# Join of a hybrid decoder layer: residual rows turned in pairs of blocks, the last output products and the first MLP products put in one fixed TensorE order

## The chip, the cores and the metric

The kernel runs on one core of one Trainium2 chip. The metric is device time in microseconds (us) from the launch's first to its last work on the core; lower is better. The core has TensorE (PE; its weight loads are shown as PEld), VectorE (DVE), ScalarE (ACT), GpSimd (POOL), and SyncE (SP), which here issues nearly all transfers.

## The reference

One decoder layer on 512 tokens of width 1024, with 16 meta tokens ahead of them. What matters here is the place where the two mixing branches meet:

```python
merged = jax.nn.sigmoid(gate_att) * att + jax.nn.sigmoid(gate_rwkv) * rw
h = layer_norm(ALPHA * h + merged @ w_out[l], ln1_g[l], ln1_b[l])
ff = jnp.square(jax.nn.relu(h @ w_ff1[l])) @ w_ff2[l]
h = layer_norm(ALPHA * h + ff, ln2_g[l], ln2_b[l])
```

`att` is windowed attention, `rw` a recurrent time mix over 16 heads, `w_out` is 1024x1024, `w_ff1` 1024x4096 and `w_ff2` 4096x1024.

## The kernel before, in words

All large products keep f32 accuracy by splitting both operands into a rounded high part and a remainder (`whi`/`wlo`, `hhi`/`hlo`, `h1hi`/`h1lo`) and adding three matmuls, high by high, low by high and high by low. A weight tile (128x1024, 512 KB) is read from memory into one of two `wraw` buffers (line 267), rounded by ACT in two halves (L258) and its remainder taken by DVE in two halves (L261). There are three `whi`/`wlo` pairs and a few `wk` tiles that are kept longer. A tile's buffer comes free when its last reader is done, so a weight load waits for DVE, a rounding for PE.

The layer runs as stages over eight pairs of heads (`s` = -1 to 8). In each stage `weave` lays a list of items, each with a due time in us, between the matmuls of "units" (a projection each). TensorE's order is written out this way (`manual_schedule`); the other engines' orders are made by a scheduler from priorities (`ahead(n)` raises one) and are then fixed lists too. Each engine works its list strictly in order.

The last stage (`s == PAIRS`) holds the last pair's recurrence, the second half of its attention (`attend(s - 1, t1=1.0)[4:]`: two turns of the score rows `pt<-sb`, L1160, and the products `av`, L1180), the residual rows `h` rebuilt and written out (L1247, L1248), and, as units, the output projection: `out_unit` computes `acc[b, n]` (traced as `o`, L1273 to L1275), the rows of block `b` (128 tokens) and half `n` of the columns, over the first six of the eight contraction tiles (`q` = 0 to 2, two tiles each). The last two tiles (`q` = 3) need the last pair's merged heads and come behind the stage.

There the join starts: for each block the four last `project_out` steps (L1273 to L1275), and interleaved with them `first_norm(b)`: add the residual (L1522), statistics (L1503, L1511), 1/deviation (L225, and POOL at L226), normalise (L1527), turn the block's 128x1024 rows into columns by eight transposes in two PSUM banks (L1533), scale and shift on ACT (L1536, eight of 128x128), round on ACT (`h1hi`, L1541, two), remainder on DVE (`h1lo`, L1542, two). The first `NORMED = 2` blocks are normed between the output products. From here to the end TensorE's order is the scheduler's.

Then come the MLP's products `up` (L331 to L333): for `f` = 0 to 2 (`SPLITF = 3`) the first 256 tokens and then the second 256, so that work can start when two blocks are normed; all other `f` take 512 tokens at once. Block 3 is normed behind the first two. ReLU and square are at L1581 to L1584. The tiles `zw`, `za`, `sghi`, `sglo` (pool `lz`, read by the low-rank products and the gate) are given back ahead of the join.

Of the kernel before, what the change touches and what calls it, by code (L numbers as in the profile page):

```python
# [78 lines left out]
NORMED = 2  # L79
# [52 lines left out]
def hybrid_layer_kernel(ctx: ExitStack, tc: tile.TileContext, I: dict, out: bass.AP):  # L132
# [32 lines left out]
    p1 = ctx.enter_context(ExitStack())  # L165
    lz = p1.enter_context(tc.tile_pool(name="lz", bufs=1))
# [84 lines left out]
    def split(raw, hi=None, lo=None, n=P):  # L251
        if hi is None:
            hi = wst.tile([P, D], F32R, name="whi", tag="whi", bufs=WB[0])
            lo = wst.tile([P, D], F32R, name="wlo", tag="wlo", bufs=WB[1])
        w = D // 2
        for q in range(2):
            qs = slice(q * w, (q + 1) * w)
            act.copy(hi[:n, qs], raw[:n, qs])  # L258
        for q in range(2):
            qs = slice(q * w, (q + 1) * w)  # L260
            dve.tensor_tensor(lo[:n, qs], raw[:n, qs], hi[:n, qs].bitcast(F32), op=ALU.subtract)  # L261
        return hi, lo

    def load(tiles, i, keep=None):

# [152 lines left out]

        return dense(col, spans, evict, after=lambda: after(s["z"]))

    zw = lz.tile([P, T], F32R, name="zw")
    za = lz.tile([P, T], F32R, name="za")
    sghi = lz.tile([P, SEQ], F32R, name="sghi")
    sglo = lz.tile([P, SEQ], F32R, name="sglo")

    rest = CONST.shape[1]
    nc.sync.dma_start(con[:, w0:rest], I["consts"][:, w0:rest])
# [836 lines left out]
    def load_out(q, n):  # L1264
        wout[q, n] = load("w_out", 2 * q + n)

    def project_out(q, n, b, d):
# [6 lines left out]
        pe.matmul(acc[b, n], mhi[k][:, bs], lo[:, ws], start=False, stop=False)  # L1274
        pe.matmul(acc[b, n], mlo[k][:, bs], hi[:, ws], start=False, stop=last)  # L1275

    def out_unit(n, blocks, asks):

        if n == 0 and blocks[0] == 0:
# [5 lines left out]
        for q in range(KT // 2 - 1):  # L1285
# [4 lines left out]
            if asks[q]:  # L1290
                load_out(*asks[q])


    SS = [{} for j in range(PAIRS)]
# [161 lines left out]
    p1.close()  # L1456
    prw.close()
    fin = ctx.enter_context(tc.tile_pool(name="fin", bufs=1))

# [55 lines left out]
    h1hi = fin.tile([P, KT, SEQ], F32R, name="h1hi")  # L1515
    h1lo = fin.tile([P, KT, SEQ], F32R, name="h1lo")

    def first_norm(b):
        bs = slice(b * P, (b + 1) * P)
        for n in range(2):  # L1520
            ns = slice(n * 512, (n + 1) * 512)
            dve.scalar_tensor_tensor(  # L1522
                res[b][:, ns], res[b][:, ns], ALPHA, acc[b, n], op0=ALU.mult, op1=ALU.add
            )
            half_stats(st1, b, n)
        mean, r = moments(st1, b)
        dve.tensor_scalar(res[b], res[b], mean, r, op0=ALU.subtract, op1=ALU.mult)  # L1527
        for q in range(2):
            tp = new_bank(b, q, "tp")
            full = fin.tile([P, 4, P], F32, name="h1f", tag="h1f", bufs=2)  # L1530
            for d in range(4):
                k = 4 * q + d
                pe.transpose(tp[:, d * P : (d + 1) * P], res[b][:, k * P : (k + 1) * P], ident)  # L1533
            for d in range(4):
                k = 4 * q + d
                act.activation(  # L1536
                    full[:, d, :], tp[:, d * P : (d + 1) * P], AF.Identity,
                    bias=vcol("ln1_b", k), scale=vcol("ln1_g", k),
                )
            ks = slice(4 * q, 4 * q + 4)  # L1540
            act.copy(h1hi[:, ks, bs], full)  # L1541
            dve.tensor_tensor(  # L1542
                h1lo[:, ks, bs], full, h1hi[:, ks, bs].bitcast(F32), op=ALU.subtract
            )

    for b in range(4):
        for n in range(2):
            for d in range(2):
                project_out(KT // 2 - 1, n, b, d)
        if 0 < b <= NORMED:  # L1550
            with ahead(400):
                first_norm(b - 1)
    pps.close()
    pa = ctx.enter_context(tc.tile_pool(name="pa", bufs=1, space=PSUM))
    ffp = ctx.enter_context(tc.tile_pool(name="ffp", bufs=1))


    def finish(b):
# [6 lines left out]
    NF = DFF // P // 2  # L1565
    for half in range(2):
        fx = [ffp.tile([P, NF - KT, SEQ], F32R, name="f" + x, tag="f" + x) for x in ("hi", "lo")]
        fhi, flo = (m + [f[:, k, :] for k in range(NF - KT)] for m, f in zip((mhi, mlo), fx))

        def up(f, w, t0, n, pool_):  # L1570
            hi, lo = w
            ps = pool_.tile([P, 512], F32, name="dps", tag=f"acc{f % 4}")
            ts_ = slice(t0, t0 + n)
            for k in range(KT):
                ks = slice(k * P, (k + 1) * P)
                three(
                    ps[:, :n], hi[:, ks], lo[:, ks], h1hi[:, k, ts_], h1lo[:, k, ts_],
                    first=(k == 0), last=(k == KT - 1),
                )
            r = fin.tile([P, SEQ], F32, name="rl", tag="rl", bufs=2)[:, :n]  # L1580
            act.activation(r, ps[:, :n], AF.Relu)  # L1581
            act.activation(fhi[f][:, ts_], r, AF.Square)
            dve.tensor_tensor(r, r, r, op=ALU.mult)
            dve.tensor_tensor(flo[f][:, ts_], r, fhi[f][:, ts_].bitcast(F32), op=ALU.subtract)  # L1584

        split_f = SPLITF if half == 0 else 0
        if half == 0:

            for b in range(NORMED, 3):
                first_norm(b)  # L1590
            ws = [load("w_ff1", f, ffp if f > 1 else None) for f in range(split_f)]
            for f in range(2):
                up(f, ws[f], 0, SEQ // 2, pa)
            first_norm(3)
            ppr.close()
            pb = ctx.enter_context(tc.tile_pool(name="pb", bufs=1, space=PSUM, side="right"))
            for f in range(2, split_f):
                up(f, ws[f], 0, SEQ // 2, pa)
            for f in range(split_f):
                up(f, ws[f], SEQ // 2, SEQ // 2, pa)  # L1600
        for f in range(split_f, NF):
            up(f, load("w_ff1", half * NF + f), 0, SEQ, pb)
            if half == 0 and f in (6, 10):

                row = rowvec(("ln1_g", "ln1_b")[f // 10], wst, "wraw")
# [70 lines left out]
```

## Time and profile before

| | us |
|---|---|
| median of 3 runs | 999.57 |
| lowest and highest | 995.95, 1003.83 |
| profiled execution | 997.59 |
| its span, first to last instruction | 995.8 |
| PE busy in it | 946.2 |
| DVE busy | 654.3 |
| ACT busy | 469.6 |
| last stage with the first six tiles of the output products | about 556 to 616 |
| join, to the end of `f` = 3 of the first MLP products | about 616 to 660 |

PE is busy for 95% of the span, so only the places where it waits, or runs at a lower granted clock, can give time. A row of the timeline shows the start, the duration, the engine, the line and operation, and in brackets the engine's idle time just before it with what ended it. Matmuls overlap: rows 0.39 us long that start every 0.23 us are a full PE.

### The profile page before, as it was taken

The page shows a single profiled execution, that of the slowest core. Times are in us where ns is not written, and L with a number is a line of the kernel's source. Part 1 is how long each engine was busy: PE and PEld are TensorE (multiplying, and loading weights), DVE is VectorE, ACT ScalarE, POOL GpSimd, SP SyncE. Part 2 cuts the span into 40 slices and gives each one's busy share as a digit, 9 for nine tenths or more (in the row PEclk, how much of TensorE's full clock was granted, in tenths as well). Part 3 has the DMA queues.
Part 4 walks back from the last instruction along what each step waited for, and adds up shares of the span by engine and source line. Part 5 has one row for each costly group of instructions (what it writes and reads, how often), then busy time and mean ns, then how long its engine had stood idle before and what let it go on. Part 6 is the DMA issues. An engine that isn't in the chain of part 4 may idle for free.

```text
span 995.8 us, 19206 instructions
## 1 busy us (share of the span) xinstructions
PE 946.2 (95%) x7533; PEld 790.8 (79%) x7533; DVE 654.3 (66%) x1503; ACT 469.6 (47%) x1238; POOL 43.4 (4%) x108
## 2 busy tenths in 40 slices
PE   4999899999999999999998999899999999999996
PEld 3988788888888887878886677788888888888885
DVE  8577688787887878778867865766433234543437
ACT  6535448465584575745736822843422124442220
POOL 2000000010010000100001000100000000000001
PEclk9999899999999999999999999899999999999999
DMA  7544332433224432233444535133232323323232
GB/s 269 94 126 125 99 81 67 126 76 104 76 50 124 104 112 68 70 109 88 129 124 104 171 106 212 64 106 127 86 106 74 117 86 104 95 95 100 71 105 84
DMA packets 82674, 105.47 MB, mean 106 GB/s; under 512 B 47766, under 2 KB 54664, under 8 KB 82584
## 3 DMA queue, kind: packets, MB, share of 16 engines
q1 hardware_dynamic: 81088, 102.16, 35.1%
q10 hardware_dynamic: 1496, 2.08, 0.6%
q8 instruction: 59, 0.97, 0.4%
q14 instruction: 31, 0.25, 0.1%
HBM read 86.29 MB, written 13.74 MB: 100 GB/s over the span
## 4 chain that ended last, share of the span: by engine, by line
PE 69%; DVE 17%; ACT 8%; issue 2%; DMA 2%; SPq 0%; POOL 0%; DVEq 0%; ACTq 0%; POOLq 0%
PE dps L331 12%; PE dps L332 11%; PE dps L333 11%; PE acc L1486 6%; PE acc L1488 6%; PE acc L1487 6%; DVE wlo L261 2%; ACT Z L744 2%; PE sc L659 2%; PE o L1273 2%; PE av L1180 2%; DVE AX L884 2%; PE o L1275 1%; PE o L1274 1%; DVE Xf L768 1%
## 5 line engine op out<-in xcount | busy, mean ns | idle before, releaser
L261 DVE TENSOR_TENSOR wlo<-wraw,whi 128x512 fp32r<-128x512 f32 x242 | 159.4, 685 | 175.3 <-ACT whi L258 174.9
L258 ACT CAST whi<-wraw 128x512 fp32r<-128x512 f32 x242 | 141.8, 618 | 274.3 <-PE dps L332 135.2
L331 PE MATMUL dps<-hhi,whi 128*128 128x264 f32 (+1 forms) x640 | 219.1, 342 | 3.4 <-DVE ftmp L764 1.4
L332 PE MATMUL dps<-hlo,whi 128*128 128x264 f32 (+1 forms) x640 | 204.9, 320 | 1.4 <-DVE hlo L312 1.4
L333 PE MATMUL dps<-hhi,wlo 128*128 128x264 f32 (+1 forms) x640 | 204.1, 319 | 0.4 <-DVE wlo L261 0.4
L331 PEld LDWEIGHTS dps<-hhi,whi 128*128 128x128 f32 x640 | 121.8, 190 | 17.1 <-issue 3.0
L333 PEld LDWEIGHTS dps<-hhi,wlo 128*128 128x128 f32 x640 | 121.4, 190 | 9.1 <-DVE wlo L261 0.6
L332 PEld LDWEIGHTS dps<-hlo,whi 128*128 128x128 f32 x640 | 121.8, 190 | 6.9 <-DVE hlo L312 2.5
L331 PE MATMUL dps<-h1hi,whi 128*128 128x512 f32 (+1 forms) x264 | 100.1, 380 | 3.8 <-ACT h1f L1536 3.8
L332 PE MATMUL dps<-h1lo,whi 128*128 128x512 f32 (+1 forms) x264 | 100.3, 380 | 0.0
L333 PE MATMUL dps<-h1hi,wlo 128*128 128x512 f32 (+1 forms) x264 | 99.9, 379 | 0.0
L331 PEld LDWEIGHTS dps<-h1hi,whi 128*128 128x128 f32 x264 | 50.4, 191 | 12.9 <-ACT h1f L1536 4.1
L332 PEld LDWEIGHTS dps<-h1lo,whi 128*128 128x128 f32 x264 | 50.4, 191 | 9.3 <-DVE h1lo L1542 0.2
L333 PEld LDWEIGHTS dps<-h1hi,wlo 128*128 128x128 f32 x264 | 50.4, 191 | 9.1
L1486 PE MATMUL acc<-whi,hhi 128*128 128x512 f32 x128 | 50.7, 396 | 0.0
L1488 PE MATMUL acc<-whi,hlo 128*128 128x512 f32 x128 | 50.4, 394 | 0.0
L1487 PE MATMUL acc<-wlo,hhi 128*128 128x512 f32 x128 | 50.0, 391 | 0.0
L1486 PE MATMUL acc<-whi,fhi 128*128 128x512 f32 x112 | 43.6, 389 | 0.0
L1487 PE MATMUL acc<-wlo,fhi 128*128 128x512 f32 x112 | 43.6, 389 | 0.0
L1488 PE MATMUL acc<-whi,flo 128*128 128x512 f32 x112 | 43.6, 389 | 0.0
L897 ACT ACTIVATE Z<-ch,PC 64x64 f32<-64x64 f32 x56 | 17.3, 308 | 45.6 <-DVE Z L895 44.3
L744 ACT COPY Z<-vt 64x64 f32<-64x64 f32 x128 | 26.4, 206 | 9.0 <-PE vt L737 7.6
(292 smaller groups left out, 1721.9 us busy)
## 6 DMA issues: line engine op xcount, KB each, us to landing
wraw<-in_w_ff_dram SPq DMA_DIRECT2D x64, 512.0 KB, 3.6
wraw<-in_w_in_dram SPq DMA_DIRECT2D x52, 512.0 KB, 4.1
wraw<-in_w_out_dram SPq DMA_DIRECT2D x8, 512.0 KB, 3.8
xt<-in_x_dram SPq DMA_DIRECT2D x4, 512.0 KB
Nd<-NT SPq DMA_DIRECT2D x16, 128.0 KB, 3.0
bv<-bv SPq DMA_DIRECT2D x8, 256.0 KB
bvm<-bv SPq DMA_DIRECT2D x8, 256.0 KB, 3.4
qs<-qhi SPq DMA_DIRECT2D x16, 128.0 KB, 4.0
```

What stands on the lines that cost most here:

```text
L258: act.copy(hi[:n, qs], raw[:n, qs])
L261: dve.tensor_tensor(lo[:n, qs], raw[:n, qs], hi[:n, qs].bitcast(F32), op=ALU.subtract)
L331: pe.matmul(ps, whi, xhi, start=first, stop=False)
L332: pe.matmul(ps, whi, xlo, start=False, stop=False)
L333: pe.matmul(ps, wlo, xhi, start=False, stop=last)
L659: pe.matmul(scs[e][:, c * P : (c + 1) * P], BK[ER[e], 4 * i + c, :], AXg[ER[e], e, 4 * i + c], start=True, stop=True,)
L744: act.copy(Z[2 * i + cc][64 * (1 - e) : 64 * (1 - e) + 64, e, :], vt[64 * cc : 64 * cc + 64, i * P + e * HD : i * P + (e + 1) * HD],)
L884: dve.tensor_tensor(AXg[:, e, cs], AXg[:, e, cs], gqs[e].rearrange("p (c k t) -> p c k t", c=4, k=2), op=ALU.add,)
L1180: pe.matmul(av[64 * e : 64 * e + 64, (2 * i + n) * P : (2 * i + n + 1) * P], vs[:, 2 * i + n], ps[:, 2 * n + e, :], start=(d == 0), stop=( ...
L1486: pe.matmul(acc[b], xhi[k][:, bs], hi[:, ws], start=first, stop=False)
L1487: pe.matmul(acc[b], xhi[k][:, bs], lo[:, ws], start=False, stop=False)
L1488: pe.matmul(acc[b], xlo[k][:, bs], hi[:, ws], start=False, stop=last)
```

## The change

1. In the last stage the second half of attention is due at 3.0 instead of 1.0 (`t1`), so that its first turn stands behind more output products.
2. The unit of blocks 2 and 3, columns 1, takes the blocks as 3, 2 and ends after four contraction tiles instead of six; the other two come in the join.
3. The weights of MLP product `f` = 0 are loaded in the last stage (`first_up`, due at 17.0) into the four tiles of `lz`, whose pool is kept; this load is ahead of the last two loads of `w_out` in SP's queue. `f` = 1 goes to `wk` tiles, 2 and 3 to `whi`/`wlo` (`SPLITF = 4`).
4. The join is one TensorE order: last products of blocks 0 and 1, the four left over of unit 3, last products of 2 and half of 3, the 16 transposes of blocks 0 and 1 (`turn_rows(0)`), the rest of block 3, then for `f` = 0 to 3 the first 256 tokens with the contraction in two halves; the transposes of blocks 2 and 3 stand in the middle of the second halves.
5. Two blocks share a PSUM bank in the turn, so that ACT's scale and shift take 128x256 (32 become 16) and the roundings cover two contraction tiles of 256 tokens. Blocks 0 and 1 are normalised on ACT (`add_norm`, L1546 of the new file) with one added small DVE step, blocks 2 and 3 on DVE as before.

```diff
-SPLITF = 3
+SPLITF = 4
...
+    def load_pieces(tiles, i, pieces):
+
+        raw = wst.tile([P, D], F32, name="wraw", tag="wraw", bufs=WB[2])
+        nc.sync.dma_start(raw, I[tiles][i])
+        for q in range(2):
+            hi, lo = pieces[0][q], pieces[1][q]
+            qs = slice(q * (D // 2), (q + 1) * (D // 2))
+            act.copy(hi, raw[:, qs])
+            dve.tensor_tensor(lo, raw[:, qs], hi.bitcast(F32), op=ALU.subtract)
+        return pieces
...
-        (1, (2, 3), ((3, 0), (3, 1), None)),
+        (1, (3, 2), ((3, 0), (3, 1))),
...
-                items += attend(s - 1, t1=1.0)[4:] + join(s - 1, 25.5)
+                items += attend(s - 1, t1=3.0)[4:] + join(s - 1, 25.5)
                 items += [(2.0, (), F(merged, s - 2)), (25.6, (), F(merged, s - 1))]
-                items += [(3.0, (), residual_gain)]
+                items += [(3.0, (), residual_gain), (17.0, (), first_up)]
...
+            if b < 2:
+                nm = fin.tile([P, 1], F32, name="fnm", tag=f"fnm{b}")
+                dve.tensor_scalar(nm, mean, r, -1.0, op0=ALU.mult, op1=ALU.mult)
+                act.activation(res[b], res[b], AF.Identity, bias=nm, scale=r)
+            else:
+                dve.tensor_scalar(res[b], res[b], mean, r, op0=ALU.subtract, op1=ALU.mult)
...
+                for d in range(2):
+                    for b in range(2):
+                        pe.transpose(
+                            t4[:, d, b * P : (b + 1) * P],
+                            res[2 * u + b][:, (k + d) * P : (k + d + 1) * P], ident,
+                        )
+                for d in range(2):
+                    act.activation(
+                        full[:, d], t4[:, d], AF.Identity,
+                        bias=vcol("ln1_b", k + d), scale=vcol("ln1_g", k + d),
+                    )
+                act.copy(h1hi[:, k : k + 2, us], full)
...
+        for b in range(2):
+            last_rows(b, 0)
+            last_rows(b, 1)
+        for d in range(2):
+            for b in (3, 2):
+                project_out(KT // 2 - 2, 1, b, d)
+        last_rows(2, 0)
+        last_rows(2, 1)
+        last_rows(3, 0)
+        turn_rows(0)
+        last_rows(3, 1)
...
+        for f in range(SPLITF):
+            up(ps[f], ws[f], first, range(KT // 2))
+        for f in range(SPLITF):
+            if f == 1:
+                turn_rows(1)
...
+            up(ps[f], ws[f], first, range(KT // 2, KT))
+            squared(f, ps[f], first, n)
...
+        for f in range(SPLITF):
+            ps = pb.tile([P, 512], F32, name="dps", tag=f"acc{f}")[:, :n]
+            up(ps, ws[f], second, range(KT))
+            squared(f, ps, second, n)
```

On TensorE, at the start of the last stage, before (`o` with a number is one block's bank, `pt<-con,sb` the turn of the score rows, `up` and `meta` the recurrence):

```order
L1160 MATMUL pt<-con,sb 128x128 x4
L1273 MATMUL o_7692<-whi,hhi 128x512
L1274 MATMUL o_7692<-wlo,hhi 128x512
L1275 MATMUL o_7692<-whi,hlo 128x512
L820 MATMUL up<-XB,U 16x16 x32
L917 MATMUL meta<-RHm,XTm 16x64 x2
L1273 MATMUL o_7693<-whi,hhi 128x512
L1274 MATMUL o_7693<-wlo,hhi 128x512
L1275 MATMUL o_7693<-whi,hlo 128x512
```

On TensorE at the same place, now, from the same `up` on:

```order
L829 MATMUL up<-XB,U 16x16 x32
L926 MATMUL meta<-RHm,XTm 16x64 x2
L1282 MATMUL o_7693<-whi,hhi 128x512
L1283 MATMUL o_7693<-wlo,hhi 128x512
L1284 MATMUL o_7693<-whi,hlo 128x512
L1282 MATMUL o_7692<-whi,hhi 128x512
L1283 MATMUL o_7692<-wlo,hhi 128x512
L1284 MATMUL o_7692<-whi,hlo 128x512
L1169 MATMUL pt<-con,sb 128x128 x4
L844 MATMUL up<-X_7739,NT 32x32 x16
L931 MATMUL meta<-SVm,BTm 64x64 x2
```

The turn moved from ahead of `up<-XB` to behind two steps of output products that follow it, and one step of output products more now stands ahead of `up<-XB`; the recurrence's next step, `up<-X`, follows the turn at once.

On ScalarE at the join, before (`wk` and `whi` are weight roundings, `h1f` the scale and shift, `h1hi` its rounding):

```order
L258 CAST wk<-wraw 128x512 x2
L1536 ACTIVATE h1f<-tp,vc 128x128 x5
L1541 CAST h1hi<-h1f 128x4x128
L1536 ACTIVATE h1f<-tp,vc 128x128 x4
L1541 CAST h1hi<-h1f 128x4x128
```

On ScalarE at the join, now:

```order
L256 CAST wk<-wraw 128x512 x2
L1546 ACTIVATE res_8163<-res_8163,fnm,rsf_8226 128x1024
L256 CAST whi<-wraw 128x512 x2
L1546 ACTIVATE res_8164<-res_8164,fnm,rsf_8250 128x1024
L256 CAST whi<-wraw 128x512
L1565 ACTIVATE h1f<-tp,vc 128x256 x3
L1569 CAST h1hi<-h1f 128x2x256
L1565 ACTIVATE h1f<-tp,vc 128x256
L256 CAST whi<-wraw 128x512
L1569 CAST h1hi<-h1f 128x2x256
```

The two normalisations came to ScalarE, and the roundings of `f` = 2 and 3 now stand between them and the first columns.

On VectorE in the join, now (`res` with a number is a block's residual rows, 8165 block 2 and 8166 block 3):

```order
L1538 SCALAR_TENSOR_TENSOR res_8166<-res_8166,o_7890 128x512
L1526 BN_AGGR fmv<-fst_8173 128x2
L259 TENSOR_TENSOR wlo<-wraw,whi 128x512
L223 TENSOR_SCALAR rsf_8286<-fmv 128x1
L1518 BN_STATS fst_8174<-res_8166 128x6
L1548 TENSOR_SCALAR res_8165<-res_8165,fmv,rsf_8286 128x1024
L1570 TENSOR_TENSOR h1lo<-h1f,h1hi 128x2x256
L1538 SCALAR_TENSOR_TENSOR res_8166<-res_8166,o_8104 128x512
L1570 TENSOR_TENSOR h1lo<-h1f,h1hi 128x2x256
```

The first remainder of the turned rows, `h1lo`, stands behind block 2's normalisation.

More of the change, by code (lines that the diff above doesn't have):

```diff
@@ L78 @@
 HOLD = 4
-NORMED = 2
 SBB = 2
 WB = (3, 3, 2)
-SPLITF = 3
+SPLITF = 4
 PS = (2, 2, 1, 1, 2)
@@ L164, in hybrid_layer_kernel @@
     hpool = ctx.enter_context(tc.tile_pool(name="hpool", bufs=1))
-    p1 = ctx.enter_context(ExitStack())
-    lz = p1.enter_context(tc.tile_pool(name="lz", bufs=1))
+    lz = ctx.enter_context(tc.tile_pool(name="lz", bufs=1))
     prw = ctx.enter_context(ExitStack())
@@ L419, in shifted @@
         return dense(col, spans, evict, after=lambda: after(s["z"]))
[L421 to L424, printed above, removed]
+    zw = lz.tile([P, T], F32R, name="zw", tag="zw")
+    za = lz.tile([P, T], F32R, name="za", tag="za")
+    sghi = lz.tile([P, SEQ], F32R, name="sghi", tag="sghi")
+    sglo = lz.tile([P, SEQ], F32R, name="sglo", tag="sglo")
     rest = CONST.shape[1]
@@ L1275, in project_out, with first_up @@
         pe.matmul(acc[b, n], mlo[k][:, bs], hi[:, ws], start=False, stop=last)
+    def first_up():
+        A["w1"] = load_pieces("w_ff1", 0, [
+            [lz.tile([P, SEQ], F32R, name="w1", tag=t) for t in tags]
+            for tags in (("zw", "za"), ("sghi", "sglo"))
+        ])
     def out_unit(n, blocks, asks):
-        if n == 0 and blocks[0] == 0:
+        if n == 0 and 0 in blocks:
             with ahead(PRI["dense"]):
@@ L1284, in out_unit @@
             acc[b, n] = new_bank(b, n, f"o{b}{n}")
-        for q in range(KT // 2 - 1):
+        for q, ask in enumerate(asks):
             for d in range(2):
@@ L1289, in out_unit @@
                     yield 3 * 0.227
-            if asks[q]:
-                load_out(*asks[q])
+            if ask:
+                load_out(*ask)
     SS = [{} for j in range(PAIRS)]
@@ L1455, in hybrid_layer_kernel @@
     p2.close()
-    p1.close()
     prw.close()
@@ L1516, in hybrid_layer_kernel @@
     h1lo = fin.tile([P, KT, SEQ], F32R, name="h1lo")
[L1518 to L1523, printed above, removed]
-            )
[L1525 to L1555, printed above, removed]
+    def add_norm(b):
+        with ahead(400):
+            for n in range(2):
+                ns = slice(n * 512, (n + 1) * 512)
+                dve.scalar_tensor_tensor(
+                    res[b][:, ns], res[b][:, ns], ALPHA, acc[b, n], op0=ALU.mult, op1=ALU.add
+                )
+                half_stats(st1, b, n)
+            mean, r = moments(st1, b)
+            if b < 2:
[4 more added lines that the diff above has]
+                dve.tensor_scalar(res[b], res[b], mean, r, op0=ALU.subtract, op1=ALU.mult)
@@ new lines, in turn_rows @@
+    def turn_rows(u):
+        us = slice(u * 2 * P, (u + 1) * 2 * P)
+        with ahead(400):
+            for k in range(0, KT, 2):
+                tp = new_bank(2 * u + k // 2 % 2, k // 4, "tp")
+                t4 = tp.rearrange("p (d t) -> p d t", d=2)
+                full = fin.tile([P, 2, 2 * P], F32, name="h1f", tag="h1f", bufs=2)
+                for d in range(2):
[8 more added lines that the diff above has]
+                        bias=vcol("ln1_b", k + d), scale=vcol("ln1_g", k + d),
+                    )
+                act.copy(h1hi[:, k : k + 2, us], full)
+                dve.tensor_tensor(
+                    h1lo[:, k : k + 2, us], full, h1hi[:, k : k + 2, us].bitcast(F32),
+                    op=ALU.subtract,
+                )
@@ new lines, in hybrid_layer_kernel, with activations, up @@
+    NF = DFF // P // 2
+    ffp = ctx.enter_context(tc.tile_pool(name="ffp", bufs=1))
+    def activations():
+        fx = [ffp.tile([P, NF - KT, SEQ], F32R, name="f" + x, tag="f" + x) for x in ("hi", "lo")]
+        return (m + [f[:, k, :] for k in range(NF - KT)] for m, f in zip((mhi, mlo), fx))
+    fhi, flo = activations()
+    def up(ps, w, ts_, ks):
+        for k in ks:
+            if isinstance(w, list):
+                c = slice(k % 4 * P, (k % 4 + 1) * P)
+                hi, lo = (x[k // 4][:, c] for x in w)
+            else:
+                hi, lo = (x[:, k * P : (k + 1) * P] for x in w)
+            three(
+                ps, hi, lo, h1hi[:, k, ts_], h1lo[:, k, ts_],
+                first=(k == 0), last=(k == KT - 1),
+            )
@@ L1563, in finish @@
             (nc.sync, nc.scalar)[q].dma_start(out[0, b * P : (b + 1) * P, qs], res[b][:, qs])
-    NF = DFF // P // 2
     for half in range(2):
[L1567 to L1602, printed above, removed]
+        if half:
+            fhi, flo = activations()
+        for f in range(0 if half else SPLITF, NF):
+            ps = pb.tile([P, 512], F32, name="dps", tag=f"acc{f % 4}")
+            up(ps, load("w_ff1", half * NF + f), slice(0, SEQ), range(KT))
+            squared(f, ps, slice(0, SEQ), SEQ)
             if half == 0 and f in (6, 10):
```

20 lines of the change are left out of this document (added).

## Prediction

> **What bounds the kernel now.** First the page, for the share of each engine:
>
> ```profile
> PE 946.2 (95%) x7533; PEld 790.8 (79%) x7533; DVE 654.3 (66%) x1503; ACT 469.6 (47%) x1238; POOL 43.4 (4%) x108
> ```
>
> TensorE sets the end, and the change leaves nearly all of its work as it is. So it can save only what TensorE loses between 560 and 660 us, the stretch that it reorders. The waits of TensorE there, all of them (total, times, longest):
>
> ```profile
> PE dps L331 <- ACT h1f L1536: 3.8, 1, 3.8
> PE pt L1160 <- ACT sb L1150: 2.0, 1, 2.0
> PE o L1273 <- ACT z L975: 0.9, 1, 0.9
> ```
>
> That is 6.7 us. Behind a wait the granted clock can fall. The busy times by window (the column behind POOL is the granted clock) and one shorter wait from an earlier stage:
>
> ```profile
> 486.80:490.20 3.40, 1.85 (x9) 1.19 (x9) 3.31 (x9) 3.37 (x10) 0.00 (x0) 1.00 0.27 88
> 562.70:566.50 3.80, 1.80 (x8) 1.07 (x7) 3.80 (x9) 3.80 (x11) 0.00 (x0) 0.94 0.60 180
> 566.50:569.80 3.30, 3.30 (x75) 2.32 (x74) 3.24 (x7) 2.65 (x10) 0.00 (x0) 0.55 0.88 254
> 628.50:632.30 3.80, 0.02 (x1) 0.03 (x1) 3.78 (x8) 3.80 (x11) 0.00 (x0) 0.82 0.02 10
> 632.30:637.70 5.40, 5.40 (x25) 5.40 (x26) 4.96 (x12) 3.25 (x8) 1.48 (x2) 0.50 0.31 95
> ...
> 488.41 0.91 PE L1160 MATMUL pt<-con,sb 128*128 128x128 f32 x3 [1.55 <-ACT sb L1150]
> ```
>
> The wait of 3.8 us was followed by 5.4 us at half clock, that of 2.0 us by 3.3 us at about half (0.55); the wait of 1.55 us at 488 left the clock at 1.00. So two of the three waits cost about double.
>
> **The change part by part.**
>
> *The start of the last stage (`t1` 1.0 to 3.0).* TensorE's rows:
>
> ```profile
> 562.34 0.39 PE L1275 MATMUL o<-whi,hlo 128*128 128x512 f32 x1
> 564.73 1.21 PE L1160 MATMUL pt<-con,sb 128*128 128x128 f32 x4 [2.00 <-ACT sb L1150]
> 570.24 0.69 PE L835 MATMUL up<-X,NT 32*32 32x32 f32 x32
> 571.13 0.44 PE L1180 MATMUL av<-pall,vtok 128*64 128x128 f32 x4
> 572.15 0.66 PE L1160 MATMUL pt<-con,sb 128*128 128x128 f32 x4
> 572.57 0.48 PE L1273 MATMUL o<-whi,hhi 128*128 128x512 f32 x1
> ```
>
> Matmuls of 512 columns start every 0.23 us, so a step of output products (three) is 0.69. A turn of four is 0.42 (572.15 to 572.57), an `up` with its `meta` 0.89 (570.24 to 571.13). From 562.57, when the next instruction could start, to 570.24 the kernel before does one turn, three steps and one `up` with `meta`: 0.42 + 2.07 + 0.89 = 3.4 us of work in 7.7, so 4.3 lost. Now the same pieces stand in the order step, `up`, step, step, turn, and then `up<-X` follows. What they wait for, on ACT and DVE:
>
> ```profile
> 562.72 1.65 ACT L258 CAST whi<-wraw 128x512 fp32r<-128x512 f32 x3
> 564.28 1.87 ACT L1150 ACTIVATE sb<-sb,sm 128x128 f32<-128x128 f32 x6
> 567.74 1.10 ACT L826 COPY XB<-up 16x128 f32<-16x128 f32 x4
> 568.86 0.41 ACT L919 COPY SVm<-meta 16x64 f32<-16x64 f32 x2
> ...
> 568.23 0.89 DVE L830 STREAM_TRANSPOSE X<-XB 32x256 f32<-32x256 f32 x2
> ```
>
> TensorE reaches the turn at 562.57 + 3 x 0.69 + 0.89 = 565.5. ACT is free of roundings at 564.3 and has four `sb` done (0.30 each) at 565.5: the wait of 2.0 goes. But ACT now does `XB` next (1.1, to 566.6), DVE turns it 0.3 later (566.9; before, 568.84 to 569.12), and TensorE is through its turn at 566.0: a new wait of 0.9 at `up<-X`. ACT then has four more `sb` (567.8) and `SVm` (568.0) ahead of the second `meta`, for which TensorE is ready at 567.5: 0.4 to 0.5. Together 1.35 are left of 4.3; both are shorter than the 1.55 that left the clock alone. Gain **2.9**; at the bounds 4.3 (neither wait) and 1.0 (both waits, and a fall of the clock: 3.3 us at half speed lose 1.65, plus 0.3).
>
> *The bank behind `z`.* The next fence holds the rest of TensorE's rows that I use. At 606.86 an `o` waits for ACT to read its bank. Now block 3's step, whose bank is free, stands ahead and covers 0.69 of the 0.93: gain **0.7**.
>
> ```profile
> 606.86 0.50 PE L1273 MATMUL o<-whi,hhi 128*128 128x512 f32 x1 [0.93 <-ACT z L975]
> 627.37 1.09 PE L1533 MATMUL tp<-con,res 128*128 128x128 f32 x8
> 632.28 0.58 PE L331 MATMUL dps<-h1hi,whi 128*128 128x256 f32 x1 [3.81 <-ACT h1f L1536]
> 637.76 0.28 PE L333 MATMUL dps<-h1hi,wlo 128*128 128x256 f32 x1
> 641.35 0.28 PE L333 MATMUL dps<-h1hi,wlo 128*128 128x256 f32 x1
> 641.48 1.03 PE L1533 MATMUL tp<-con,res 128*128 128x128 f32 x8
> 642.27 0.37 PE L331 MATMUL dps<-h1hi,wk 128*128 128x256 f32 x1
> 654.18 0.40 PE L331 MATMUL dps<-h1hi,whi 128*128 128x512 f32 x1
> 659.65 0.39 PE L331 MATMUL dps<-h1hi,whi 128*128 128x512 f32 x1
> ```
>
> *The wait at the join.* Before, TensorE is out of work after the turn at 627.37, and ACT has 16 `h1f` to do. Now I count from T, the start of block 0's last products, with these durations:
>
> ```profile
> 622.12 1.14 ACT L258 CAST wk<-wraw 128x512 fp32r<-128x512 f32 x2 [5.43 <-DMA wraw<-in_w_ff_dram]
> 624.98 1.85 ACT L1536 ACTIVATE h1f<-tp,vc 128x128 f32<-128x128 f32 x5 [1.72 <-PE tp L1533]
> 627.99 1.28 DVE L1522 SCALAR_TENSOR_TENSOR res<-res,o 128x512 f32<-128x512 f32 x2
> ...
> L1527 DVE TENSOR_SCALAR res<-res,fmv,rsf 128x1024 f32<-128x1024 f32 x4 | 3.2, 811 | 0.5 <-POOL rsf L226 0.4
> L241 ACT ACTIVATE xt<-xt,nm,rs 128x1024 f32<-128x1024 f32 x2 | 2.4, 1227 | 0.0
> L1581 ACT ACTIVATE rl<-dps 128x256 f32<-128x256 f32 x6 | 2.4, 393 | 1.3 <-PE dps L333 1.3
> L226 POOL TENSOR_TENSOR rsf<-rsf,mhalf 128x1 f32<-128x1 f32 x4 | 2.6, 648 | 31.7 <-PE o L1275 19.4 <-DVE rsf L225 12.3
> ```
>
> TensorE: 18 steps end at T + 12.5, 16 transposes (eight are 0.79, 641.48 to 642.27) at 14.1, two steps at 15.5. The normalised block 1 is there in time: its second sum can start at 5.7, its statistics end at 8.5; DVE then waits for `f` = 2's rounding, whose buffer is read until 8.4, and ACT (1.23 for a normalisation) has block 1 done at 11.9. The columns: ACT rounds half of `f` = 3 when the 18th step has freed its buffer (12.7 to 13.3), then three `h1f` at 0.4 and `h1hi` at 0.5: 15.1, ahead of 15.5. DVE is later. At 10.7 it turns to block 2, and with 0.6 for each 128x512 (two in 1.28) it does: two sums, the second when its products end at 11.4 (12.1), two statistics (13.3), a sum (13.9), aggregate and `wlo` (14.6), 1/deviation and a statistic (15.3, POOL's 0.65 beside it), the normalisation (0.81; 16.2), and only then `h1lo`: 16.8. `up`'s second matmul waits for it, 1.3 us; the third contraction tile waits 0.5 more for the next `h1lo`, which stands behind one more sum. From there nothing is late by this count (the second turn is reached at 24.4, block 3 is normalised at 22.7). So 1.8 of 3.8 stay: gain **2.0**, bounds 3.8 and, with DVE a whole wait of 3.8 late, 0.
>
> *The clock behind it.* 632.28 to 637.76 are 5.5 us for 16 matmuls of 256 columns (0.12 each) and eight transposes (0.79): 2.7 us of work. Without the long wait the **2.8** are back; bounds 2.8 and 0.
>
> *Two MLP halves more.* `f` = 3 now takes 48 matmuls at 0.12 for 24 in 5.47 us (654.18 to 659.65): −0.3. Four interruptions by transposes become two, about 0.2 each by the rows around them: +0.4. Net **0.1**. The Trainium skill (TensorE: Matmul & The Clock Gate, Back-to-back issue gap) gives sustained 81 ns at 128 columns and 131 ns at 512; a straight line puts 256 near 98, an estimate from that page, and the split at 24 x (196 − 131) = 1.6 us against the change. By that the sum would be 7.2; the rows above decide for 0.3.
>
> *The early load.* `f` = 0 is issued ahead of two loads that have over 8 us to spare; its two roundings (1.14) now stand in ACT's list ahead of the chain's last step:
>
> ```profile
> 597.50 0.31 ACT L897 ACTIVATE Z<-ch,PC 64x64 f32<-64x64 f32 x1 [0.82 <-DVE Z L895]
> ...
> 598.59 0.63 PE L951 MATMUL Y<-Z,AX 128*64 128x64 f32 x14
> wraw<-in_w_ff_dram SPq DMA_DIRECT2D x7, 512.0 KB, 4.2
> ```
>
> They take up the 0.82 us of idle time and 0.3 more; the reader comes 0.8 after `Z` ends. Cost nothing; if the load came a microsecond late, half of that would show.
>
> Sum: 2.9 + 0.7 + 2.0 + 2.8 + 0.1 = 8.5 us. The profiled execution (997.59) would become 989.1. It lies 2.0 below the median of 999.57, inside the spread of the runs, so the forecast for the median is **991.1**.
>
> **The rivals.**
>
> *The clock falls again at the join.* The two new waits, 1.3 and 0.5, lie within 2.6 us of each other, and 1.8 in one stretch is between the 1.55 that was harmless and the 2.0 that was not. Then 3.3 to 5.4 us run at half speed and 1.65 to 2.7 are lost: 992.8 to 993.8. For it: how close 1.8 is to 2.0. Against it: the clock fell only behind waits in one piece. The Trainium skill (same page, Why this matters for your kernels) says that gaps up to about 3 us leave the clock alone. By that this rival could not be. The trace differs: 2.0 us were enough at 564.7.
>
> *The start does not do what it says*: the wait for `sb` only moves to `XB` and `SVm`, and the clock falls there too: the gain is 1.0 for 2.9, so 993.0.
>
> *The count is too careful*: DVE gets to `h1lo` in time and both waits of the stage's start vanish: 991.1 − 1.8 − 1.4 = 987.9.
>
> *Slower than before: ACT's list blocks.* The half rounding of `f` = 3 stands ahead of the first `h1f`. Its load is issued only when DVE has finished `f` = 1 (T + 7.9), and must land by T + 12.7, 4.8 later, where such loads took 4.2. Each microsecond beyond holds up `h1f`, `h1hi`, `h1lo` and TensorE by one, and from about one on the clock falls as well (2.8). It decides from a landing 5.7 us too late, when 5.7 + 2.8 use up the 8.5; at 17 us too late the kernel would stand at 1011. Against it: the transfers have room there, since DMA moved 10 GB/s from 628.5 to 632.3 (the last column of its row).
>
> **How the numbers follow.** As worked out 0.50 (988 to 994, with the spread of runs); clock at the join 0.20; the start gains little 0.13; too careful 0.12; ACT blocked 0.05. The likeliest is 991.1. A median of a few runs moves by some 3 us (the runs lie 3.6 below to 4.3 above theirs), so the range goes from the too careful case less 3, 985, to the two clock cases together (995.7) and a little more, 997. One per cent, about what a measurement here can tell from no change, is 10 us: faster by more needs under 989.6, which the too careful case gives nearly always (0.11), the likeliest in four of ten (0.20), the others sometimes (0.06). Slower by over 1% is the far end of the last case, 0.04. Rounded: 0.37, 0.59, 0.04.
>
> **What would show it.** Right: no wait over 1.5 us on TensorE from 560 to 660, and the clock at 1.00 there; `up<-X` waits for DVE's `X` about 0.9; the first `up` of the MLP waits for `h1lo`, 1 to 1.5; `f` = 4 starts some 8.5 us earlier than 659.65. Wrong: a wait of TensorE on a rounding or a load in the join, a clock of 0.5 behind it, or time lost elsewhere, where the order is unchanged.

## The result

| | median of 20 runs | lowest to highest | profiled execution | its span |
|---|---|---|---|---|
| before | 996.99 us | 994.04 to 1003.83 | 997.59 us | 995.8 us |
| after | 995.92 us | 992.13 to 999.29 | 996.54 us | 994.7 us |

The ratio is 0.9988, with a 95% interval of 0.9977 to 0.9999: about 1 us less, where 991.1 and a gain of 8.5 us in the profiled execution were forecast. The 991.1 set out from 999.57, the median of the three runs that were known of the kernel before; its median over 20 runs is 2.6 lower.

### The profile page after: what moved, and what is told of

It is laid out like the page before. It is cut to its first block, busy times and chain, and to the rows that moved or that the text cites. A ratio compares the mean times of both kernels' runs of the same rounds, so it can differ in the third digit from the quotient of the medians.

```text
span 994.7 us, 19253 instructions
## 1 busy us (share of the span) xinstructions
PE 949.3 (95%) x7557; PEld 790.0 (79%) x7557; DVE 653.1 (66%) x1505; ACT 468.8 (47%) x1226; POOL 44.2 (4%) x108
## 4 chain that ended last, share of the span: by engine, by line
PE 67%; DVE 17%; ACT 9%; DMA 3%; issue 2%; POOL 0%; SPq 0%; DVEq 0%; ACTq 0%; POOLq 0%
PE dps L340 12%; PE dps L341 11%; PE dps L342 11%; PE acc L1501 6%; PE acc L1503 6%; PE acc L1502 6%; DVE wlo L259 2%; ACT Z L753 2%; PE sc L668 2%; PE av L1189 2%; DVE AX L893 2%; PE o L1282 1%; DVE ftmp L773 1%; DVE Xf L777 1%; PE o L1284 1%
## 5 line engine op out<-in xcount | busy, mean ns | idle before, releaser
L341 PE MATMUL dps<-h1lo,whi 128*128 128x512 f32 (+1 forms) x256 | 97.5, 381 | 0.0
L340 PE MATMUL dps<-h1hi,whi 128*128 128x512 f32 (+1 forms) x256 | 97.4, 381 | 0.0
L342 PE MATMUL dps<-h1hi,wlo 128*128 128x512 f32 (+1 forms) x256 | 97.4, 381 | 0.0
L342 PEld LDWEIGHTS dps<-h1hi,wlo 128*128 128x128 f32 x256 | 48.1, 188 | 10.1
L340 PEld LDWEIGHTS dps<-h1hi,whi 128*128 128x128 f32 x256 | 48.1, 188 | 10.0
L341 PEld LDWEIGHTS dps<-h1lo,whi 128*128 128x128 f32 x256 | 48.1, 188 | 10.0
L1601 DVE TENSOR_TENSOR rl<-rl 128x512 f32<-128x512 f32 (+1 forms) x36 | 22.8, 632 | 15.4 <-ACT hhi L1600 9.2
```

Of the source, the lines that this page charges most:

```text
L340: pe.matmul(ps, whi, xhi, start=first, stop=False)
L341: pe.matmul(ps, whi, xlo, start=False, stop=False)
L342: pe.matmul(ps, wlo, xhi, start=False, stop=last)
```

## The profile after

First TensorE's waits from 560 to 660 us in the changed kernel, all of them (total, times, longest). They answer to the three of before:

```profile
PE dps L341 <- DVE h1lo L1570: 1.4, 2, 1.1
PE up L844 <- DVE X L839: 0.7, 2, 0.5
PE meta L931 <- ACT SVm L928: 0.4, 1, 0.4
PE dps L340 <- ACT h1f L1565: 0.3, 1, 0.3
PE o L1282 <- ACT z L984: 0.2, 1, 0.2
```

3.0 us in place of 6.7, and with the same partners as forecast: `up<-X` behind DVE's `X`, `meta` behind `SVm`, the first `up` of the MLP behind `h1lo`. TensorE's own rows (start, duration, the wait in brackets) at the stage's start, at the join, and at the first matmul of `f` = 4:

```profile
565.47 0.60 PE L1169 MATMUL pt<-con,sb 128*128 128x128 f32 x4
566.61 0.22 PE L844 MATMUL up<-X,NT 32*32 32x32 f32 x2 [0.55 <-DVE X L839]
566.99 0.69 PE L844 MATMUL up<-X,NT 32*32 32x32 f32 x30 [0.16 <-DVE X L839]
568.06 0.33 PE L931 MATMUL meta<-SVm,BTm 48*64 48x64 f32 x4 [0.39 <-ACT SVm L928]
...
627.86 0.38 PE L341 MATMUL dps<-h1lo,w 128*128 128x256 f32 x1 [1.13 <-DVE h1lo L1570]
...
653.33 0.40 PE L340 MATMUL dps<-h1hi,whi 128*128 128x512 f32 x1
```

`f` = 4 starts 6.3 us earlier than the 659.65 of before; 8.5 was forecast. The windows (the granted clock is the column behind POOL's busy time) show one half of what is missing there:

```profile
565.44:568.85 3.41, 2.32 (x43) 1.75 (x42) 3.07 (x7) 3.24 (x11) 0.00 (x0) 1.00 0.97 279
568.85:572.26 3.41, 3.41 (x38) 2.42 (x37) 2.87 (x6) 1.83 (x6) 0.00 (x0) 0.50 0.27 104
631.00:638.00 7.00, 7.00 (x63) 7.00 (x63) 3.32 (x7) 2.94 (x8) 0.93 (x1) 1.00 0.50 153
```

At the join the clock stays at 1.00, as forecast (by the clock records from 572.26 to 992.10 us). At the stage's start it falls, though no wait there is longer than 0.55 us. By the starts of four matmuls in the two timelines, the time between them, stage by stage:

```
                                                      before    after    gained   forecast
up to the first output product (561.09, 560.82)                           0.3       -
first product to the 37th (581.34, 580.10)             20.25    19.28     1.0      2.9
37th to block 0's last products (615.28, 610.66),
  less the 12 products (2.8 us) that now stand later   33.94    33.33     0.6      0.7
from there to f = 4, less the same 12                  44.36    39.89     4.5      4.9
f = 4 to the last matmul (987.77, 986.66)             328.12   333.33    -5.2       -
```

So 6.3 us are gained, and 5.2 of them are given back behind 653 us, where the order of work is the old one, TensorE is busy without a gap and the clock is at 1.00 in both. TensorE in the second half of the MLP, before and then after, 50 us by windows (busy time and number of matmuls):

```profile
830.00:880.00 50.00, 50.00 (x222) 41.42 (x221) 25.16 (x38) 21.45 (x39) 0.00 (x0) 1.00 0.30 95
```

```profile
830.00:880.00 50.00, 50.00 (x216) 40.24 (x215) 24.08 (x36) 20.48 (x36) 0.00 (x0) 1.00 0.28 92
```

Six matmuls fewer in the same time. And four in a row, before and then after:

```profile
839.91 0.39 PE L333 MATMUL dps<-h1hi,wlo 128*128 128x512 f32 x1
840.14 0.39 PE L331 MATMUL dps<-h1hi,whi 128*128 128x512 f32 x1
840.37 0.39 PE L332 MATMUL dps<-h1lo,whi 128*128 128x512 f32 x1
840.60 0.39 PE L333 MATMUL dps<-h1hi,wlo 128*128 128x512 f32 x1
```

```profile
839.76 0.39 PE L341 MATMUL dps<-h1lo,whi 128*128 128x512 f32 x1
839.99 0.40 PE L342 MATMUL dps<-h1hi,wlo 128*128 128x512 f32 x1
840.23 0.39 PE L340 MATMUL dps<-h1hi,whi 128*128 128x512 f32 x1
840.46 0.40 PE L341 MATMUL dps<-h1lo,whi 128*128 128x512 f32 x1
```

They start 0.227 us apart before, and 0.23 to 0.24 after. There is no wait in it: a row shows it only in the distance to the next.

What differs is where the tiles lie. `lz` is now never closed, so everything that is allocated behind it lies 8320 bytes higher (two tiles of 528 elements and two of 512, of 4 bytes each; 128 modulo 256), and some small tiles add to that. The place of the tiles in the built programs, modulo 256 bytes (the theory that the experiments test; the traces hold no addresses), with the mean distance of the 512-column matmuls from `f` = 4 on:

```
         weights   h1   f, wk   `up` on h1   last products on f   on merged heads
before     224     224   224     0.2267           0.2267              0.2317
after      224      96   160     0.2329           0.2294              0.2317
```

672 matmuls x 0.0062 + 383 x 0.0027 = 5.2 us: all that was given back.

## The experiments: where the tiles lie

The numbers say in which order they ran.

**1. The pool alone.** The kernel before, with `lz` left open and nothing else:

```diff
-    p1 = ctx.enter_context(ExitStack())
-    lz = p1.enter_context(tc.tile_pool(name="lz", bufs=1))
+    lz = ctx.enter_context(tc.tile_pool(name="lz", bufs=1))
...
-    p1.close()
```

> The kernel before, with one thing of the change: the pool `lz` stays open, so that `h1hi`, `h1lo`, `fhi`, `flo` and `wk` lie 8320 bytes higher; the order of work is the old one. Theory (place): the MLP's matmuls of 512 columns go slower because of where their tiles lie, whatever ran ahead of them: those that read `h1` start 0.232 to 0.233 us apart, not 0.2267, and the kernel takes 4.3 to 6.7 us more than before (4.3 from `h1` alone, 2.4 more if `f` and `wk`, which are now 128 bytes off the weights modulo 256 as `h1` is, do the same). Rival (order): the spacing comes from what the new order of work sets going, its halves and buffers: 0.2267 and no change here. Rival (chance): it differs from one execution to the next: no change on the median.

Measured: 1005.16 us, ratio to before 1.0083 (1.006 to 1.0107), some 7.7 us slower between the medians. The same 50 us:

```profile
830.00:880.00 50.00, 50.00 (x215) 40.20 (x215) 23.70 (x37) 20.06 (x37) 0.00 (x0) 1.00 0.30 95
```

`up` on `h1` is at 0.2329, the last products on `f` (now 128 bytes off the weights, too) at 0.2324; together 6.5 us over 0.2267, inside the interval of 6.0 to 10.7. With the old order, and so without a gain to set against it, the pool costs what the MLP loses. The order of work has no part in it.

**2. The changed kernel, with the tiles put back.**

```diff
+    fin.tile([P, 32], F32, name="gap0")
     h1hi = fin.tile([P, KT, SEQ], F32R, name="h1hi")
...
+    ffp.tile([P, 48], F32, name="gap1")
     fhi, flo = activations()
```

> The changed kernel with two unused tiles of 128 and 192 bytes, ahead of `h1hi` and of `fhi`, which put `h1`, `f` and `wk` on the same place modulo 256 as the weights, as they lay before. Place: spacing of the MLP's matmuls on `h1` and `f` back at 0.2267 us, 5.2 us less than the changed kernel, about 6.3 under the one before: 990.7. Order or chance: spacing 0.232 as in the changed kernel, 996.

Measured: 990.73 us, ratio 0.9941 (0.9923 to 0.996); both distances are 0.2267, and the 50 us hold as many matmuls as before the change:

```profile
830.00:880.00 50.00, 50.00 (x222) 41.40 (x221) 24.84 (x38) 20.68 (x37) 0.00 (x0) 1.00 0.32 96
```

320 bytes that nobody uses bring the change's own gain out.

**3. Everything moved together.** The kernel before:

```diff
+    cst.tile([P, 16], F32, name="gap0")
     wst = ctx.enter_context(tc.tile_pool(name="wst", bufs=2))
```

> The kernel before with an unused tile of 64 bytes ahead of the weights' pool: weights, `hhi`, `hlo`, `h1`, `f` and `wk` all move up by 64 bytes together. Place, in the form that the distance between the two operands of a matmul modulo 256 decides: spacing as before (0.2267 on `h1` and `f`, 0.231 on `hhi`), no change. Place, in the form that each tile's own address decides: slower spacing on `h1` and `f`, 3 to 6 us more.

Measured: 997.91 us, ratio 1.0005 (0.9987 to 1.0023); distances 0.2267, 0.2267 and 0.2317 as before. A shift of 64 bytes that both operands share changes nothing, so it is the place of one against the other that counts, and neither's own.

**5. The merged heads**, on top of the kernel of experiment 2. They lay in rows of 528 elements (2112 bytes), so that the blocks' places modulo 256 go round by 64:

```diff
-    mhi = [hhi[:, k, NMETA:] for k in range(KT)]
-    mlo = [hlo[:, k, NMETA:] for k in range(KT)]
+    mhi, mlo = (
+        [x.rearrange("p k t -> p (k t)")[:, k * SEQ : (k + 1) * SEQ] for k in range(KT)]
+        for x in (hhi, hlo)
+    )
```

> The kernel of the second experiment (changed, `h1` and `f` on the weights' place modulo 256), and the merged heads, too, which are kept in the tiles of `hhi` and `hlo`, now in rows of 512 elements from the tile's start (2048 bytes apart) in place of rows of 528 (2112 apart): every block of them lies on the weights' place modulo 256. Place: the matmuls on them go from 0.2317 to 0.2267 us, 1.9 us less over the MLP's 384, and some 0.8 less over the 192 output products ahead of it: 988.0. Rival: only the tiles' starts matter, not each row's, or what holds up these products is the change of operand tiles from one to the next: 990.7 as in the second experiment.

Measured: 988.62 us, ratio 0.9907 (0.9884 to 0.9929). The last products on the heads are at 0.2267, too (0.2317): the whole MLP now runs at one distance. Twelve us of it, here and in the kernel with the tiles put back:

```profile
730.00:742.00 12.00, 12.00 (x55) 9.94 (x54) 2.59 (x4) 2.28 (x4) 0.00 (x0) 1.00 0.34 113
```

```profile
730.00:742.00 12.00, 12.00 (x53) 9.77 (x52) 3.28 (x6) 2.95 (x6) 0.00 (x0) 1.00 0.30 87
```

The output products ahead of the join gained only 0.2 of the 0.8 expected (from 572 us on, 0.2300 for 0.2317 between products that follow each other), though their rows were moved as well: what holds them up besides is open.

**7. Another distance**, on top of the kernel of experiment 2, one run: the unused tiles at 192 and 320 bytes.

> The kernel of the second experiment with the unused tiles at 192 and 320 bytes, so that `h1` lies 64 bytes behind the weights modulo 256 and `f` and `wk` 192. One look for the spacing by distance, of which 0 and 128 for `h1`, 0, 64 and 128 for `f` are known. Place modulo 256 in any distance: 0.229 to 0.233 on both, 2.5 to 7 us over the second experiment in all. If only 128 bytes apart collide: 0.2267 on both; if places modulo 128 collide, which 64 and 192 share: the same spacing on both.

Measured: 993.27 us. `up` on `h1`, 64 bytes off, is at 0.2289. `f`, 192 bytes behind the weights and so 64 ahead modulo 256, lies where it lies in the changed kernel (160) and showed the same 0.2294, so it says nothing new. In the three distances seen the cost grows: 0.2267 at 0, 0.229 at 64 to either side, 0.233 at 128. It does not give every size: the merged heads of 2112 bytes a row go round by 64, and the mean of the four distances would be 0.2295, where 0.2317 was measured.

## The experiments: the join, the start and the clock

**4. The start alone.** The kernel before with `t1=3.0` in place of 1.0.

> The kernel before with `t1=3.0` for 1.0 alone. By the prediction's count the last stage gains 2.9 us. By its rival 1.0. A third view, from the changed kernel's trace, where the waits went as counted and the clock fell all the same: 2.9 where the clock's window (3.4 us, running on its own) happens not to fall on the stage's sparse stretch, 1.2 where it does, so 1.2 to 2.9 on the median. The MLP's spacing is as before.

Measured: 995.34 us, ratio 0.9981 (0.9963 to 0.9999), about 2 us less. Its waits in the stretch, of which the last two replace the 2.0 for `sb`:

```profile
PE dps L331 <- ACT h1f L1536: 3.8, 1, 3.8
PE o L1273 <- ACT z L975: 0.9, 1, 0.9
PE up L835 <- DVE X L830: 0.7, 2, 0.5
PE meta L922 <- ACT SVm L919: 0.4, 1, 0.4
```

**6. The join without the start.** The kernel of experiment 2 with `t1=1.0`.

> The kernel of the second experiment with `t1` back at 1.0, so the join and the early load without the new start. By the prediction's sum the start is worth 2.9: 993.6. By the fourth experiment's median it is worth 2.1: 992.8. If the two gains share the same clock window or the join gives its part only with the new start: 995 or more.

Measured: 992.86 us, ratio 0.9962 (0.9947 to 0.9976): by the ratio the join is worth 3.8 us (2.4 to 5.3; the medians lie 4.7 apart), where 0.7 + 2.0 + 2.8 + 0.1 = 5.6 were forecast, and the start 992.86 − 990.73 = 2.1 on top, between medians of different rounds.

**What makes the clock fall.** The same wait of 1.55 us for `sb` in the stage before, on which the forecast rested since it left the clock at 1.00, ends in half clock in the kernel of experiment 2:

```profile
487.43 1.21 PE L1169 MATMUL pt<-con,sb 128*128 128x128 f32 x4 [1.55 <-ACT sb L1159]
```

```profile
485.62:489.04 3.42, 1.86 (x9) 1.05 (x8) 3.24 (x11) 3.39 (x11) 0.00 (x0) 1.00 0.27 79
489.04:492.45 3.41, 3.41 (x10) 2.66 (x9) 3.14 (x5) 1.39 (x4) 0.00 (x0) 0.50 0.80 276
```

In the clock records of every trace all changes lie on a grid of 3.413 us that runs through the execution, and begins at another phase in each: in the profile of before they are at 112.08, 566.05, 630.90 and 637.73, and 637.73 − 112.08 is 154.0 x 3.413. So I counted, in each stretch of the grid at full clock, the columns of the matmuls that start in it, as a share of 8192 (a yardstick: products of 512 columns 0.2267 us apart make 0.94 on the mean). In the first nine profiles, from 45 to 980 us:

```
share of 8192 columns   stretches   followed by half clock
under 0.36                  27              27
0.36 to 0.43                19               2
over 0.43                 2379               0
```

The bounds 0.36 and 0.43 were read off these same nine profiles; the three of experiments 8 to 10 are the test, and are told there and at the end. The wait of 1.55 us shows the phase at work: in the profile of before an edge of the grid at 487.54 cuts through it, and the two stretches have 0.63 and 0.50; in the kernel of experiment 2 it lies inside one, which has 0.25.

The stretch 565.44 to 568.85 above has 0.34: a turn, 32 products of 32 columns, and the waits. Busy time doesn't tell it: TensorE is busy for 2.3 of its 3.4 us. The old join leaves under 0.2 in one stretch of all four profiles that have it, and the clock fell in all four; the new one leaves at least 0.38, and it fell in none of the five that have it.

**8. Filling the idle time.** On top of the kernel of experiment 5, products that nothing reads, in three places where TensorE waits:

```diff
+    def fill(ps, n, cols):
+        for i in range(n):
+            pe.matmul(ps[:, :cols], hhi[:, 0, :P], hhi[:, 1, :cols], start=True, stop=True)
...
+                if j == 0:
+                    fill(up, 14, 512)
...
+                if j == PAIRS - 1:
+                    fill(up[:, 256:512], 4, 256)
...
+        if j == PAIRS - 2 and i == 0:
+            fill(pt, 6, 512)
```

> The kernel of the fifth experiment with idle time of TensorE filled at three places by products that nothing reads, written to the bank of the instruction that waits: 14 of 512 columns (3.2 us) ahead of the first `up<-X`, which waits 3.8 us at 110.9 for a transfer; 6 of 512 (1.4 us) ahead of the turn at 489 that waits 1.6 for `sb`; 4 of 256 (0.5 us) ahead of the `up<-X` of the last stage that waits 0.55. Theory (columns): the clock is set on a grid of 3.413 us by the columns that TensorE streamed in the stretch before; in the nine profiles so far all 27 stretches below 0.36 of what a stretch can hold were followed by half clock, 2 of 19 between 0.36 and 0.43, and none of 2379 above. The fills lift these places over 0.43, so that no half clock follows at 107 to 118, 489 to 493 and 566 to 573; what is left is one early fall at 60 to 75 in some executions, and the end. A stretch at half clock costs 1.4 us by the spread of the runs, and about 2.5 of them go: 985, 3 to 4 us under the fifth experiment. Rival (waits): only the length of a wait in one piece counts; then 566 still falls in some executions, and the gain is the same or less. Rival (work): more products are more work, and no faster: 988.6 or more.

Measured: 986.13 us, ratio 0.9877 (0.9855 to 0.9898). The clock is at 1.00 from 31 to 979 us, where the work ends (the column behind POOL's busy time):

```profile
31.00:979.00 948.00, 925.91 (x7499) 777.01 (x7497) 628.67 (x1447) 452.11 (x1194) 37.88 (x79) 1.00 0.36 103
```

The four runs lie within 1.0 us of each other, the six of experiment 5 within 5.3. Against experiment 5 the time is 2.5 us less between the medians, but the two intervals overlap. One stretch at 71.6 went on at full clock with 0.30, the only one under 0.36 that did. The second place is no test here: its products ran elsewhere (see 10), and the stretch of that wait, unfilled, happened to have 0.44.

**9. Busy, but with few columns.** The same three places with 56, 24 and 8 products of 16 columns.

> The same three fills with products of 16 columns, 56, 24 and 8 of them, which keep TensorE as busy for about as long (some 0.055 us each, as the products of 128 columns in the trace), and stream an eighth of the columns or less. Columns: the clock falls as without the fill, at 107 to 118 always and at 489 and 566 to 573 in some executions, 988.6 as in the fifth experiment. Waits or busy time: no fall there, and the time of the filled kernel.

Measured: 993.78 us, ratio 0.9951 (0.9935 to 0.9966). In the first place, TensorE without a gap and at half clock for three stretches:

```profile
108.21:111.62 3.41, 3.41 (x33) 3.41 (x32) 1.82 (x4) 1.08 (x3) 0.00 (x0) 1.00 0.78 145
111.62:121.86 10.24, 10.24 (x112) 9.28 (x112) 2.26 (x5) 0.52 (x2) 0.00 (x0) 0.50 0.23 89
```

So a TensorE that the profile calls busy doesn't hold the clock (the first stretch has 0.06); the 14 products of 512 columns in the same place did. That the time is worse than experiment 5's and not the same is, as far as the rows show, the fill's own doing: I took 0.055 us for a product of 16 columns, and the 56 took 8.3 us, where the wait was 3.8; the 24 ran at 550 and took 2.4, where nothing waits:

```profile
L804 PE MATMUL up<-hhi 128*128 128x16 f32 x56 | 8.3, 292 | 0.0
```

**10. The second fill in its right place.** In the eighth kernel those six products ran at 543, ahead of a turn that waits for nothing, and the turn at 485.60 waited its 1.55 us as ever. With `j == PAIRS - 3`:

> The kernel with the three fills, the second of which stood ahead of a turn at 543 that waits for nothing, and so was 1.4 us of added work; now it stands ahead of the turn that waits 1.55 us for `sb` in the stage before. Columns: the clock stays at 1.00 as with the first filled kernel, that turn waits 0.2 instead of 1.55, and the time is 1.4 us less: 984.7. Rival (the end of that stage is set by ACT's list and not by TensorE): 986.1 as before.

Measured: 985.02 us, ratio 0.9864 (0.9843 to 0.9885), six runs within 1.8 us. The turn's wait is 0.2, and the mean clock of the profiled execution 0.999:

```profile
PE pt L1179 <- ACT sb L1167: 0.2, 1, 0.2
```

This is the fastest version of the study. It does some 5 us of products more than the kernel of experiment 5 and takes 3.6 us less between the medians (0.9843 to 0.9885 against 0.9884 to 0.9929).

## Why the prediction was wrong

*The step that failed* is in its first paragraph: "So it can save only what TensorE loses between 560 and 660 us, the stretch that it reorders." The same sentence was used the other way round, that it can lose nothing elsewhere, although the last line of the prediction has "time lost elsewhere, where the order is unchanged" as a sign of being wrong, without a price; and of the early load, for which `lz` is kept open, the count says "Cost nothing", having looked at its queue, its roundings and its reader, and not at what lies behind the pool. What the runs show in its place: 5.2 us in the MLP, by matmuls that stand 0.233 and 0.229 us apart for 0.2267, because the tiles moved against the weights. The pool alone reproduces it (1.0083), 320 bytes of padding undo it (0.9941). With the tiles where they were, the kernel has the 991 that was forecast, but by luck: the gain is 5.9 us by the ratio of 0.9941 and 6.7 between the medians, where 8.5 were summed up, and the forecast set out from a median that 20 runs put 2.6 lower.

*The start* (2.9 forecast). The waits went as counted, and a little better: 0.7 and 0.4 are left where 0.9 and 0.4 to 0.5 were. From the first output product to the 37th the profiles without a fall of the clock there take 19.2 us (experiment 3, old start) and 17.8 (experiment 2, new start), so the start gives 1.4 like for like; those with one stretch at half clock take 20.25 before and 19.3 after, 1.0. Between the medians of runs it is 2.1 (experiments 4 and 6). The rest of the 2.9 was the clock's share, which the count took as saved because 0.55 is shorter than 1.55. That rule was wrong: the same 1.55 us ended in half clock in another execution, and what sorts the cases is the columns in a stretch of a grid that lies differently in each. The rival "the start does not do what it says" named the result (1.0) and had the reason half: the clock did fall.

*The bank behind `z`* (0.7): 0.6, with 0.2 of the wait left.

*The join and the clock behind it* (2.0 + 2.8 + 0.1): 4.5 in the profiled execution, and the waits are 1.7 where 1.8 were counted. By the ratio of the runs it is less, 3.8 (2.4 to 5.3) with the bank's share in it. The 2.8 took 5.4 us at half clock as half lost. Over 156 runs of all kernels the time moves by 7.9 us for 0.01 of mean clock, so that a stretch at half clock (0.0017) costs 1.35 us and 5.4 us of it 2.1. That in the kernel before a part of those 5.4 would have been a wait anyway, since the third turn needs block 2's normalised rows, is argued from the rows and was not tried.

*The clock rival* was near: by the columns the new join is at 0.38 to 0.58 in its sparsest stretch, in two of the five profiles inside the band of 0.36 to 0.43, where some fall. The Trainium skill (TensorE: Matmul & The Clock Gate, Part 1) has the free-running window of 3413 ns that the traces show. The prediction named that page's other rule, on gaps of up to 3 us, set it against the fall behind 2.0 us, and went by the 1.55 that did no harm, without asking where on the grid a wait lies.

*ACT's list* did not block: TensorE's one wait on ACT in the join is 0.3 us.

## What to carry to other kernels

A change to a pool's lifetime moves every tile allocated behind it: compare the addresses of both matmul operands before and after, and in the profile the distance from one matmul to the next in stages that the change doesn't touch. Waits of TensorE are worth more than their length when they make a stretch of some 3.4 us sparse. Where the clock fell here, few columns had been streamed, and products that nothing reads, put into a wait that is there anyway, can pay for themselves. A forecast for a kernel whose runs differ by 10 us, for the most part with the clock, needs the time and clock of many runs, not of three and a profiled one.

## What the runs showed of the hardware that was not expected

Matmuls of 128 x 128 weights and 512 float32r columns start 0.2267 us apart when the moving and the stationary operand begin at the same place modulo 256 bytes, 0.229 with 64 bytes between them and 0.233 with 128, at full clock and with no wait in the trace (64 behind in one profile, 64 ahead in two); moving both by 64 changes nothing. The distances then repeat in a fixed pattern (0.229 and 0.238 in turn on `h1` in the second half of the changed kernel). What collides is not shown, nor are other distances. The Trainium skill (SBUF — State Buffer, SBUF: two separate sides) says, of contention between the engines, that TensorE never waits on anyone. The trace has a case of another kind: TensorE is slowed by up to 3% by the place of its own two operands.

The clock of a stretch goes with the columns of the matmuls that start in the stretch before: in all twelve profiles, 31 of the 32 stretches under 0.36 of 8192 columns were followed by half clock, 3 of 24 between 0.36 and 0.43, and none of 3185 above. In the three profiles that the bounds were not read from it is 4 of 5 (two of these empty, behind the end of the work), 1 of 5 and none of 806. Columns weighted by the share of the array's 128 rows that a product uses sort nearly as well (under 0.33, 32 of 36 were followed by half clock, of 34 falls in all), so whether rows count too is open. A stretch at half clock costs 1.35 us of this kernel by the slope over the runs, and most of the spread between runs goes with the clock: over the 20 runs of the changed kernel time and mean clock go together with a correlation of −0.88.
